# RMS norm with ReLU: two pairs of transfers merged, one wait split, and eight rows scaled on ScalarE in place of VectorE

## The chip, the cores and the metric

One core of a Trainium2 chip. The metric is the time of one execution in microseconds (us). A "faster" or "slower" needs 2%, here 3.2 us.

## The reference

```python
batch, seq, dim = 16, 1024, 512
def reference(x, gamma, eps):            # x: normal random, fp32; gamma: ones; eps: 1e-5
    rms = np.sqrt(np.mean(x ** 2, axis=-1, keepdims=True) + eps)
    return np.maximum(x / rms * gamma, 0).astype(np.float32)
```

16,384 rows of 512 numbers are read and written once: 33.55 MB in, 33.55 MB out.

## The kernel before

Each of the 128 partitions owns 128 rows. They are handled as 8 chunks of K = 16 rows (4.2 MB each over all partitions), or 16 groups of G = 8. On-chip memory has room for 6 chunks, so chunks 6 and 7 reuse the room of 0 and 1 after those are stored. SyncE issues all transfers of x and of the output in a fixed order, which is the plan of the kernel:

```python
L, S = 0, 1                      # load, store: (kind, first row, rows)
order = [(L, 0, G), (L, G, G)] + [(L, i * K, K) for i in range(1, nslots)] + [
    (S, 0, K), (S, K, K), (L, room, K), (L, room + K, K),
    (S, 2 * K, 2 * K), (S, 4 * K, 2 * K), (S, room, K),
    (S, room + K, G), (S, room + K + G, G)]
blocks = [(0, K), (K, K), (2 * K, 2 * K), (4 * K, 2 * K), (room, K), (room + K, K)]
...
for m, (kind, a, r) in enumerate(order):       # SyncE
    if m < early: continue
    if kind == S:
        if order[m - 1][0] == L:
            nc.sync.wait_ge(*((tick, 6) if a == 0 else (done, 10)))
        nc.sync.wait_ge(done, (a + r) // G)    # VectorE has finished these rows
    elif a >= room:
        take(nc.sync, sems[order.index((S, a - room, r))], 16)   # the room is free
    transfer(m)
```

The wait for `(done, 10)`: the store of chunks 2 and 3, first after the last load, is held back until ten groups, that is chunks 0 to 4, are done.

ScalarE makes the squares and their sums row by row, and a square root per group. VectorE handles chunks 0 to 2 in a loop over groups, and the rest in whole chunks: one multiply by 1/rms, one custom pass that multiplies by gamma and clips at zero.

```python
with nc.scalar.Fori(0, ngroups) as gi:         # ScalarE
    ...                                        # 8 x (Square, accumulated), then Sqrt
...
for first, last in ((3, 3), (4, 5), (6, 7)):   # VectorE
    nc.vector.wait_ge(sq, per * (last + 1 - looped))
    whole(nc.vector.reciprocal, out=rstd[:, first * K:(last + 1) * K],
          in_=rms[:, first * K:(last + 1) * K])
    nc.vector.wait_ge(sv, steps)
    for i in range(first, last + 1):
        blk = here(i * K, K)
        whole(nc.vector.tensor_tensor, out=blk, in0=blk,
              in1=rstd[:, i * K:(i + 1) * K, None].to_broadcast([P, K, d]), op=ALU.mult)
        nc.vector.wait_ge(sv, steps)
        r = G if i == nchunks - 1 else K
        for a in range(i * K, (i + 1) * K, r):
            blk = here(a, r)
            nc.vector._custom_dve(dve_ops.TENSOR_MUL_SAT, out=blk, in0=blk,
                in1=gamma_sb[:, None, :].to_broadcast([P, r, d]),
                s0=float("inf"), s1=0.0).then_inc(done, r // G)
```

## Time and profile before

| | before |
|---|---|
| time, median of the first 3 runs | 159.94 us (159.9 to 160.0) |
| span in the profile | 158.6 us |
| busy: VectorE / ScalarE / DMA queue | 85% / 54% / 98.6% |
| bytes moved | 67.1 MB, 423 GB/s over the span |
| VectorE ends / last packet ends | 151.2 / 158.1 us |

How to read the lines of the profile: DVE is VectorE, ACT is ScalarE, SPq is SyncE's queue of transfers. A row of digits cuts the span into 40 slices; 9 is a busy share of 90% or more. The line with "issue" in it is the chain: the work that ended last, followed back from wait to wait, in shares of the span. A window line gives the stretch and its length, then the busy us and number of instructions of VectorE, ScalarE and GpSimd, the granted clock, the DMA engines' share and the GB/s.

The "GB/s" and "DMA" columns of a window count a packet where it starts, so with packets of 1 to 2.4 us a window of 1 us may read 0 and the next 2.4; longer windows are safe. The costliest groups of instructions, with line, engine, operation, operands, shapes and count, then busy us and mean ns of one:

```profile
L131 ACT ACTIVATE junk<-slots 128x512 f32 x128 | 74.4, 581 | 21.7 <-POOLq L118 17.2 <-issue 4.5
L168 DVE TENSOR_TENSOR slots<-slots,rstd 128x8192 f32<-128x8192 f32 x5 | 43.4, 8689 | 0.1
L185 DVE CUSTOM_DVE_ANT_1 slots<-slots,gamma_sb 128x8192 f32<-128x8192 f32 x4 | 34.8, 8692 | 0.5
L185 DVE CUSTOM_DVE_ANT_1 slots<-slots,gamma_sb 128x4096 f32<-128x4096 f32 x2 | 8.8, 4423 | 0.0
```

A chunk costs VectorE two passes of 8.69 us, 17.4 us, and ScalarE 11.6 us. VectorE is the slower of the two, and this is what the change works on. One wait of VectorE is in VectorE's timeline (start, length, and in brackets the idle time before and what ended it):

```profile
71.03 8.69 DVE L185 CUSTOM_DVE_ANT_1 slots<-slots,gamma_sb 128x8192 f32<-128x8192 f32 x1
80.61 0.35 DVE L168 RECIPROCAL rstd<-rms 128x32 f32<-128x32 f32 x1 [0.89 <-ACT rms L136]
81.00 8.69 DVE L168 TENSOR_TENSOR slots<-slots,rstd 128x8192 f32<-128x8192 f32 x1
```

Chunk 4 waits here for chunk 5's statistics, since one reciprocal serves both.

### The profile page before, as it was taken

How to read it: one execution, taken by the hardware profiler on the slowest of the kernel's cores; microseconds unless marked ns; L12 is line 12 of the kernel's file. 1: busy time of each engine (PE TensorE's matmuls, PEld its weight loads, DVE VectorE, ACT ScalarE, POOL GpSimd, SP SyncE). 2: the span in 40 equal slices, each digit the busy share in tenths (PEclk: the TensorE clock that was granted, in tenths of full speed). 3: DMA queues.
4: the chain of work that ended last, by engine and by line, in shares of the span. 5: the costliest groups of instructions: out<-in, count | busy, mean ns of one | idle time of the engine just before them, and what ended most of it. 6: DMA issues, size and time to landing. Idle time of an engine off the chain costs nothing.

```text
span 158.6 us, 770 instructions
## 1 busy us (share of the span) xinstructions
DVE 135.2 (85%) x76; ACT 86.3 (54%) x273; POOL 0.8 (0%) x6
## 2 busy tenths in 40 slices
DVE  0014999999999999999979999999999999999910
ACT  0388929889889989988920098898600000000000
POOL 1000000000000000000000000000000000000000
DMA  6999999999999999999999999997969969999997
GB/s 190 411 450 422 512 397 397 463 463 397 405 504 413 397 413 504 405 397 463 463 397 397 446 479 397 529 463 331 529 298 496 529 264 529 397 397 397 455 405 331
DMA packets 2312, 67.12 MB, mean 423 GB/s; under 512 B 260, under 2 KB 260, under 8 KB 264
## 3 DMA queue, kind: packets, MB, share of 16 engines
q1 hardware_dynamic: 2304, 67.11, 98.6%
q10 hardware_dynamic: 8, 0.01, 0.0%
HBM read 33.56 MB, written 33.55 MB: 423 GB/s over the span
## 4 chain that ended last, share of the span: by engine, by line
DVE 44%; ACT 27%; issue 6%; ACTq 4%; DVEq 0%; POOLq 0%
ACT junk L131 26%; DVE slots L185 22%; DVE slots L168 22%; ACTq L131 3%; ACTq L126 1%; DVE rstd L168 0%; ACT rms L136 0%; ACTq L136 0%; ACTq L139 0%; DVEq L181 0%; POOLq L118 0%
## 5 line engine op out<-in xcount | busy, mean ns | idle before, releaser
L131 ACT ACTIVATE junk<-slots 128x512 f32 x128 | 74.4, 581 | 21.7 <-POOLq L118 17.2
L185 DVE CUSTOM_DVE_ANT_1 slots<-slots,gamma_sb 128x8192 f32<-128x8192 f32 (+1 forms) x6 | 43.5, 7269 | 0.6
L168 DVE TENSOR_TENSOR slots<-slots,rstd 128x8192 f32<-128x8192 f32 x5 | 43.4, 8689 | 0.1
L154 DVE SCALAR_TENSOR_TENSOR slots<-slots,rstd,gamma_sb 128x512 f32 x48 | 32.3, 747 | 0.9 <-DVE rstd L149 0.9
L131 ACT ACTIVATION_READ_ACCUMULATOR junk<-slots x128 | 23.9, 187 | 0.0
L161 DVE TENSOR_SCALAR slots<-slots x6 | 13.8, 2294 | 0.2
L142 DVE LOAD_MASK_SELECT gamma_sb<-gseed x1 | 0.0, 14 | 8.2 <-DMA gseed<-in_gamma_dram 8.2
L136 ACT ACTIVATE rms<-ss,eps_sb x16 | 4.8, 301 | 1.8
L149 DVE RECIPROCAL rstd<-rms x6 | 1.2, 196 | 5.1 <-ACT rms L136 5.1
L124 ACT ACT_TABLE_LOAD x1 | 1.3, 1283 | 4.0 <-issue 4.0
L168 DVE RECIPROCAL rstd<-rms 128x32 f32<-128x32 f32 (+1 forms) x3 | 0.9, 315 | 0.9 <-ACT rms L136 0.9
L142 DVE STREAM_SHUFFLE gamma_sb<-gseed 128x512 f32<-128x512 f32 x1 | 0.7, 721 | 0.0
L113 POOL MEMSET gseed<- 128x512 f32 x1 | 0.5, 524 | 1.9 <-POOLq L98 1.9
L214 POOL MEMSET const-uint8-127<- 128x1 uint8 x1 | 0.1, 102 | 0.0
L214 POOL MEMSET const-bfloat16-1.0<- 128x1 bf16 x1 | 0.1, 101 | 0.0
L214 POOL MEMSET const-float32-0.0<- 128x1 f32 x1 | 0.1, 98 | 0.2 <-issue 0.2
L114 POOL MEMSET eps_sb<- 128x1 f32 x1 | 0.1, 99 | 0.0
L214 POOL MEMSET const-float32-1.0<- 128x1 f32 x1 | 0.1, 98 | 0.0
## 6 DMA issues: line engine op xcount, KB each, us to landing
slots<-in_x_dram SPq DMA_DIRECT2D x7, 4096.0 KB, 29.6
out_dram<-slots SPq DMA_DIRECT2D x3, 4096.0 KB, 15.0
slots<-in_x_dram SPq DMA_DIRECT2D x2, 2048.0 KB, 9.5
out_dram<-slots SPq DMA_DIRECT2D x2, 2048.0 KB, 7.1
out_dram<-slots SPq DMA_DIRECT2D x2, 22.2
gseed<-in_gamma_dram ACTq DMA_DIRECT2D x1, 8.0 KB
```

The costliest lines, as they stand in the source:

```text
L113: nc.gpsimd.memset(gseed, 0.0).then_inc(sem_z, 1)
L124: nc.scalar.preload_act_table(ACTF.Sqrt)
L126: with nc.scalar.Fori(0, ngroups) as gi:
L131: a = nc.scalar.activation(out=junk[:, j, :], in_=slots[:, bass.ds(base + j * d, d)], func=ACTF.Square, accum_out=ss[:, bass.ds(col + j, 1)])
L136: nc.scalar.activation(out=rms[:, bass.ds(col, G)], in_=ss[:, bass.ds(col, G)], func=ACTF.Sqrt, bias=eps_sb, scale=inv_d).then_inc(sq, 1)
L142: nc.vector.stream_shuffle(gamma_sb, gseed, [0] * 32)
L149: nc.vector.reciprocal(out=rstd[:, bass.ds(col, G)], in_=rms[:, bass.ds(col, G)]).then_inc(sv, 1)
L154: r = nc.vector.scalar_tensor_tensor(out=row, in0=row, scalar=rstd[:, bass.ds(col + j, 1)], in1=gamma_sb, op0=ALU.mult, op1=ALU.mult)
L161: nc.vector.tensor_scalar_max(out=blk, in0=blk, scalar1=0.0).then_inc(done, 1)
L168: emit(**kw).then_inc(sv, 1)
L185: nc.vector._custom_dve(dve_ops.TENSOR_MUL_SAT, out=blk, in0=blk, in1=gamma_sb[:, None, :].to_broadcast([P, r, d]), s0=float("inf"), s1=0. ...
L214: nc = _bacc.Bacc("TRN2", target_bir_lowering=False, num_devices=1)
```

## The change

The intent is fewer, larger transfers and less work on VectorE at the end. Chunks 4 and 5 load together; VectorE takes each as soon as its own statistics are there; the last 16 rows leave in one store; ScalarE, idle by then, scales the last 8 rows.

```diff
-    order = [(L, 0, G), (L, G, G)] + [(L, i * K, K) for i in range(1, nslots)] + [
+    order = [(L, 0, G), (L, G, G)] + [
+        (L, K, K), (L, 2 * K, K), (L, 3 * K, K), (L, 4 * K, 2 * K),
         (S, 0, K), (S, K, K), (L, room, K), (L, room + K, K),
-        (S, 2 * K, 2 * K), (S, 4 * K, 2 * K), (S, room, K),
-        (S, room + K, G), (S, room + K + G, G)]
+        (S, 2 * K, 2 * K), (S, 4 * K, 2 * K), (S, room, K), (S, room + K, K)]
 ...
-    for first, last in ((3, 3), (4, 5), (6, 7)):
+    half = rows - G
+    for first, last in ((3, 3), (4, 4), (5, 5), (6, 7)):
 ...
+        if last == nchunks - 1:
+            nc.scalar.wait_ge(sv, steps)
+            for a in range(half, rows):
+                row = here(a, 1)
+                m = nc.scalar.activation(out=row, in_=row, func=ACTF.Identity,
+                                         scale=rstd[:, a:a + 1])
+            m.then_inc(am, 1)
         for i in range(first, last + 1):
 ...
+            r = K
+            if i == nchunks - 1:
+                r = K - G
+                nc.vector.wait_ge(am, 1)
             (multiply of r rows in place of K; one custom pass of K rows in place of two of G)
```

More of the change, by code (lines that the diff above doesn't have):

```diff
@@ L71 @@
     sv = nc.alloc_semaphore("sv")
+    am = nc.alloc_semaphore("am")
     def here(a, r):
@@ L175 @@
         nc.vector.wait_ge(sv, steps)
+        if last == nchunks - 1:
[5 more added lines that the diff above has]
+            m.then_inc(am, 1)
         for i in range(first, last + 1):
             blk = here(i * K, K)
-            whole(nc.vector.tensor_tensor, out=blk, in0=blk,
-                  in1=rstd[:, i * K:(i + 1) * K, None].to_broadcast([P, K, d]),
+            r = K
+            if i == nchunks - 1:
+                r = K - G
+                nc.vector.wait_ge(am, 1)
+            whole(nc.vector.tensor_tensor, out=blk[:, :r, :], in0=blk[:, :r, :],
+                  in1=rstd[:, i * K:i * K + r, None].to_broadcast([P, r, d]),
                   op=ALU.mult)
             nc.vector.wait_ge(sv, steps)
-            r = G if i == nchunks - 1 else K
-            for a in range(i * K, (i + 1) * K, r):
-                blk = here(a, r)
-                nc.vector._custom_dve(
-                    dve_ops.TENSOR_MUL_SAT, out=blk, in0=blk,
-                    in1=gamma_sb[:, None, :].to_broadcast([P, r, d]),
-                    s0=float("inf"), s1=0.0).then_inc(done, r // G)
+            nc.vector._custom_dve(
+                dve_ops.TENSOR_MUL_SAT, out=blk, in0=blk,
+                in1=gamma_sb[:, None, :].to_broadcast([P, K, d]),
+                s0=float("inf"), s1=0.0).then_inc(done, per)
     take(nc.sync, done, ngroups)
@@ L193 @@
     take(nc.sync, sv, steps)
+    take(nc.sync, am, 1)
     take(nc.sync, sem_g, 16)
```

## The prediction

> **What bounds the kernel now.** I read the page's slices first, since they show which unit is never idle, then the DMA queue, and the chain last.
>
> ```profile
> DVE 135.2 (85%) x76; ACT 86.3 (54%) x273; POOL 0.8 (0%) x6
> DVE  0014999999999999999979999999999999999910
> DMA  6999999999999999999999999997969969999997
> q1 hardware_dynamic: 2304, 67.11, 98.6%
> DVE 44%; ACT 27%; issue 6%; ACTq 4%; DVEq 0%; POOLq 0%
> ```
>
> VectorE is busy 85% and the chain that ended last names it with 44% and ScalarE with 27%, so one could take VectorE for the bound. But its slices start in the third of forty and end two slices before the DMA's, while the one DMA queue in use fills 98.6% of the time of all 16 engines. The 7s and 6s in the DMA row are an artefact: a packet is booked where it starts. The window view over longer stretches (the column before the last is the DMA share, the last GB/s) shows no hole:
>
> ```profile
> 12.00:60.00 48.00, 44.86 (x60) 41.17 (x133) 0.00 (x0) 1.00 1.01 437
> 60.00:99.00 39.00, 37.77 (x8) 26.55 (x86) 0.00 (x0) 1.00 1.00 430
> 99.00:138.00 39.00, 38.71 (x6) 13.72 (x45) 0.00 (x0) 1.00 0.99 430
> 138.00:148.00 10.00, 9.96 (x3) 0.00 (x0) 0.00 (x0) 1.00 0.99 426
> 148.00:158.00 10.00, 3.15 (x1) 0.00 (x0) 0.00 (x0) 1.00 0.97 413
> ```
>
> From 12 to 148 us the share is 0.99 to 1.01 at 426 to 437 GB/s. Following the packets one by one, I find 16 always in flight from about 2.2 us until the last ends at 158.1 us, and no engine idle for more than 0.18 us between two of them. So the bound is the byte count, 67.1 MB, and the chain is misleading here: it starts from the last instruction that waited, but that wait ends with a store that stood in line behind other stores.
>
> How much room is there at the end? The timeline of the last 26 us:
>
> ```profile
> 125.06 8.69 DVE L185 CUSTOM_DVE_ANT_1 slots<-slots,gamma_sb 128x8192 f32<-128x8192 f32 x1
> 133.67 8.68 DVE L168 TENSOR_TENSOR slots<-slots,rstd 128x8192 f32<-128x8192 f32 x1
> 133.78 17.73 SPq L83 DMA_DIRECT2D out_dram<-slots  x3
> 142.38 8.76 DVE L185 CUSTOM_DVE_ANT_1 slots<-slots,gamma_sb 128x4096 f32<-128x4096 f32 x2
> ```
>
> The three stores there are issued at 133.78, 146.84 and 151.17 us, each as VectorE finishes. The trace has the store of chunk 6 landing on its 16 engines at 148.3 to 148.8 us, so the first half store has stood in line for 1.4 us when the engines reach it; it lands at 153.2 to 153.7, so the second half store has stood for 2.0 us.
>
> **What the Trainium skill says.** "DMA: Bandwidth & Descriptors", section "Where 436 GB/s comes from", gives 16 ports x 32 bytes x 850 MHz = 435.2 GB/s as the ceiling. The trace agrees: packets of 65,536 bytes take 2.418 us, that is 16 x 65,536 / 2.418 us = 433.6 GB/s. The same page, section "Anatomy of one DMA", calls the semaphore write's bubble tiny; the trace has 256 such records of 7 to 9 ns. "ScalarE: Activation LUTs", section "Table sets: the hidden batching unit", has identity in every set, so the new scaling should need no second table load; the trace of before has one load, 1.28 us, for Square and Sqrt together, and can't show Identity. "SBUF — State Buffer", section "SBUF: two separate sides", says that ScalarE has its own port and that DMA and engines don't contend. The trace agrees: VectorE's 128x8192 multiply took 8.69 us at 62.2 us beside ScalarE and 8.69 us at 81.0 us beside none.
>
> **The change, part by part.**
>
> *Packets.* In the trace, medians by packet size are 0.611 us for 16,384 bytes, 1.213 for 32,768 and 2.418 for 65,536. Doubling saves 2 x 0.611 - 1.213 = 0.009 us, and 2 x 1.213 - 2.418 = 0.008 us: about 9 ns of fixed cost a packet. Each engine carries 8 of a transfer's 128 partition rows.
> - Chunks 4 and 5 in one load: 16 packets of 1.213 become 8 of 2.418 per engine, 19.408 - 19.344 = 0.06 us less.
> - The last 16 rows in one store: 16 of 0.611 become 8 of 1.213, 9.776 - 9.704 = 0.07 us less.
> - Two transfers fewer, so two semaphore writes of 9 ns fewer per engine: 0.02 us.
> All of it lies on the path, as the engines never rest: 0.15 us off.
>
> *The merged load.* Chunk 4's rows now land with chunk 5's, at 61.4 instead of 51.8 us. ScalarE began chunk 4 only at 57.8 us, being behind, so it loses about 4 us: 61.4 + 0.4 (landing to first square, as at 22.6 to 23.0) = 61.8. It then ends group 9 near 73.2 and group 11 near 84.5 us (5.79 us a group). VectorE is on chunk 3 until 79.7, so group 9 is in time. The change also splits VectorE's wait: chunk 4 waits for group 9 only, which removes the wait for group 11 (0.89 us in the trace before the reciprocal at 80.61). One reciprocal more costs some 0.2 us. Chunk 5 starts at 97.6, long after 84.5. ScalarE idles from 80.6 to 91.0 us today, waiting for chunk 6's landing, so the 4 us end in that hole: group 12 starts at 91.0 as before.
>
> *The tail on VectorE.* It multiplies 8 rows instead of 16 in chunk 7. Half of the 8192-wide multiply costs about what the custom pass on 4096 does, 4.42 us, so 8.69 - 4.42 = 4.27 us are saved; one custom pass of 8.69 instead of two of 4.42 saves 0.15. With 0.9 gained and 0.3 lost above, VectorE should end at 151.2 - 5.0 = 146.2 us.
>
> *ScalarE's new part.* Eight instructions on 128x512. The squares take 0.58 us each, so 8 x 0.6 = 5 us, from 115.4 (the reciprocal of chunks 6 and 7) to about 120.5. VectorE needs them at 132.9. Hidden.
>
> *The sum.* None of the compute gain reaches the end, unless a store is late. Stores of chunks 2 and 3, issued at 98.5 before, come at 97.5, while the engines finish chunk 7's load at 99.6 to 100.3. Chunks 4 and 5: 115.2 against a line that lasts to 119.3. Chunk 6: 133.0 against 138.6. The last store: 146.2 against 148.1. Issue to first packet needs about 1.0 us (0.73 to 1.74 at the start, 98.54 to 99.60 later, without a hole). The smallest spare is then 1.9 us, against 1.4 before. So 159.94 - 0.15 = 159.79 us.
>
> **The rivals.**
>
> *The saved VectorE time shows: about 155 us (5 us less).* For it speak the chain, with VectorE at 44%, and its unbroken work from 81 to 151 us. Against it: the DMA share of 0.97 to 1.01 in every stretch. After VectorE's end, 4.2 MB are still to go out in one store, which alone takes 9.70 us: were the line empty at 146.2, its last packet would end at 146.2 + 1.0 + 9.7 = 156.9 on the trace's clock, only 1.2 us before the 158.1 of today; with the line lasting to 148.1 it is 157.9.
>
> *The single last store is late: 161 us or more.* The last store can't start before all 16 rows are done. Without the ScalarE help VectorE would end at 146.2 + 4.3 = 150.5 us, and with the 1 us of issue the store would start 3.4 us after the line has run dry at 148.1. So this needs ScalarE's share to fail: if its group 15 or the reciprocal slipped, or if the Identity pass took over 17 us instead of 5. The squares' rate speaks against that.
>
> *The merged load opens a hole.* If chunk 4's results came over 2 us late, the stores of chunks 2 and 3, held back until then, would leave the DMA idle at 100 us. It would take group 9 beyond 82 us, and I have it at 73. Likewise the first store doesn't depend on chunk 4: it is issued at 58.4, 3 us before the loads end.
>
> *Larger packets are slower on loads.* 65,536-byte packets occur only in stores today. In 32,768-byte packets loads and stores cost the same, so I see no reason for it; 10% more on that load would be 1.9 us.
>
> **Range and chances.** The working gives 159.8. The runs of before spread over 0.1 us and another chip may shift both kernels by some tenths, hence 159.45 to 160.15. Over 2% is 3.2 us: faster would need a byte rate that the trace never shows, slower a hole of 3 us in the line; 1% and 2%.
>
> **What the profile of after would show.** Right: a DMA share of 1 to the end, 2016 records in the queue instead of 2304 (14 transfers of 128 rows, 1792, and 14 x 16 semaphore writes, where 16 transfers gave 2048 + 256), VectorE ended near 146 us, eight ScalarE instructions of about 0.6 us by 121 us, no second table load, and the wait before chunk 4's reciprocal gone. Wrong: a DMA slice well below 9 near 61, 99 or 148 us, a load packet of 64 KB over 2.5 us, or VectorE waiting for ScalarE before the last multiply.

## The result, and the profile after

The changed kernel took 159.96 us (median of 6 runs, 159.66 to 160.18) against 159.97 us (6 runs, 159.9 to 160.29) for the kernel before. The ratio is 0.9996, with a 95% interval of 0.9983 to 1.0009: the same. Ratios are the mean time of one kernel's fast runs over that of the other's of the same rounds, so not quite the ratio of the medians.

First the page of the changed kernel, busy shares, slices, queue and chain:

```profile
DVE 130.9 (83%) x76; ACT 91.3 (58%) x281; POOL 0.8 (0%) x6
DVE  0014999999999999999999999999999999998000
DMA  6999999999999699999999999997989969999996
q1 hardware_dynamic: 2016, 67.11, 98.5%
DVE 64%; issue 9%; ACT 3%; DVEq 2%; ACTq 0%; POOLq 0%
```

VectorE's row now has three empty slices at the end instead of one, yet the span is the same 158.6 us. The 6 in the DMA row, at 51.5 to 55.5 us, comes from counting the larger packets where they start; the windows below have no hole there. The queue handles 2016 records instead of 2304, as predicted, and fills nearly the same share. The chain's shares changed wildly, from VectorE 44% and ScalarE 27% to 64% and 3%, while the time did not: two such chains are no measure of what a faster engine would bring.

The windows of the kernel after, in the same stretches as in the prediction:

```profile
12.00:60.00 48.00, 44.83 (x60) 38.97 (x126) 0.00 (x0) 1.00 1.01 437
60.00:99.00 39.00, 38.62 (x9) 28.80 (x92) 0.00 (x0) 1.00 1.00 430
99.00:138.00 39.00, 38.58 (x7) 18.71 (x53) 0.00 (x0) 1.00 0.99 430
138.00:148.00 10.00, 8.14 (x1) 0.00 (x0) 0.00 (x0) 1.00 1.05 452
148.00:158.00 10.00, 0.00 (x0) 0.00 (x0) 0.00 (x0) 1.00 0.90 387
```

Up to 138 us the rates are equal to the last digit. After that 1.05 and 0.90 average to what 0.99 and 0.97 averaged to; only the packets' starts fall differently. No stretch has a hole. The last two stretches show what was gained and where it went: VectorE worked 3.15 us after 148 us before, and none now.

VectorE's timeline from chunk 4 on, and ScalarE's new part:

```profile
79.67 0.25 DVE L169 RECIPROCAL rstd<-rms 128x16 f32<-128x16 f32 x1
79.95 8.69 DVE L169 TENSOR_TENSOR slots<-slots,rstd 128x8192 f32<-128x8192 f32 x1
...
115.47 5.01 ACT L182 ACTIVATE slots<-slots,rstd 128x512 f32<-128x512 f32 x8 [1.70 <-DVE rstd L169]
115.47 8.69 DVE L169 TENSOR_TENSOR slots<-slots,rstd 128x8192 f32<-128x8192 f32 x1
124.30 8.69 DVE L195 CUSTOM_DVE_ANT_1 slots<-slots,gamma_sb 128x8192 f32<-128x8192 f32 x1
132.91 4.42 DVE L169 TENSOR_TENSOR slots<-slots,rstd 128x4096 f32<-128x4096 f32 x1
137.45 8.69 DVE L195 CUSTOM_DVE_ANT_1 slots<-slots,gamma_sb 128x8192 f32<-128x8192 f32 x1
```

The 0.89 us of waiting at 79.7 us is gone, ScalarE's eight rows are done at 120.5 us, and VectorE never waits for them. VectorE ends at 146.15 us (before: 151.15), and the last store is issued at 146.17 us. It then stands in line until the store of chunk 6 is out, which lands at 148.2 to 148.9 us.

### The profile page after: what moved, and what is told of

Read it like the earlier page. It is cut to its first block, busy times and chain, and to the rows that moved or that the text cites. A ratio compares the mean times of both kernels' runs of the same rounds, so it can differ in the third digit from the quotient of the medians.

```text
span 158.6 us, 775 instructions
## 1 busy us (share of the span) xinstructions
DVE 130.9 (83%) x76; ACT 91.3 (58%) x281; POOL 0.8 (0%) x6
## 3 DMA queue, kind: packets, MB, share of 16 engines
q1 hardware_dynamic: 2016, 67.11, 98.5%
## 4 chain that ended last, share of the span: by engine, by line
DVE 64%; issue 9%; ACT 3%; DVEq 2%; ACTq 0%; POOLq 0%
DVE slots L195 27%; DVE slots L169 25%; DVE slots L155 11%; ACT junk L132 3%; DVEq L155 1%; DVE rstd L169 1%; DVE rstd L150 1%; ACTq L132 0%; DVEq L145 0%; ACT rms L137 0%; DVEq L150 0%; DVE slots L162 0%; DVEq L194 0%; DVEq L164 0%; ACTq L137 0%
## 5 line engine op out<-in xcount | busy, mean ns | idle before, releaser
L195 DVE CUSTOM_DVE_ANT_1 slots<-slots,gamma_sb 128x8192 f32<-128x8192 f32 x5 | 43.5, 8692 | 0.7
L169 DVE TENSOR_TENSOR slots<-slots,rstd 128x8192 f32<-128x8192 f32 (+1 forms) x5 | 39.2, 7837 | 0.1
L182 ACT ACTIVATE slots<-slots,rstd 128x512 f32<-128x512 f32 x8 | 5.0, 709 | 1.7 <-DVE rstd L169 1.7
L169 DVE RECIPROCAL rstd<-rms 128x16 f32<-128x16 f32 (+1 forms) x4 | 1.1, 270 | 0.0
```

Of the source, the lines that this page charges most:

```text
L169: emit(**kw).then_inc(sv, 1)
L182: m = nc.scalar.activation(out=row, in_=row, func=ACTF.Identity, scale=rstd[:, a:a + 1])
```

## The experiments

Two theories were put against each other. The **line theory** is the prediction's: the 16 DMA engines always have a transfer waiting, so VectorE's 5 us are spare, and a change shows only if it makes a store late. The **cancelling theory**: VectorE's chain does set the end, and the change is level only because the merged transfers cost what ScalarE's help brings. The page's chain and VectorE's 85% speak for it.

The custom VectorE pass could not be used in the experiments. All of them have this stand-in, which gives the same result as long as gamma is not negative (here it is 1):

```diff
-    nc.vector._custom_dve(dve_ops.TENSOR_MUL_SAT, out=blk, in0=blk,
-        in1=gamma_sb[...], s0=float("inf"), s1=0.0)
+    nc.vector.scalar_tensor_tensor(out=blk, in0=blk, scalar=0.0,
+        in1=gamma_sb[...], op0=ALU.max, op1=ALU.mult)
```

### The stand-in: both kernels with it

> The kernel before with the custom VectorE pass replaced by a scalar_tensor_tensor (max with 0, times gamma; the same result as gamma is all ones), because the custom form can't be run again here. Control for all later runs. Both theories: the replacement also reads two operands, so about 8.7 us per 128x8192 as the custom pass, and the time stays within 0.3 us of 159.95.

> The changed kernel with the same replacement. Both theories: within 0.3 us of the control, as the changed kernel was of the kernel before; VectorE ends near 146.2 us. If it differs from the control by more, the replacement is no fair stand-in.

The control (the kernel before with the stand-in) took 160.14 us, ratio 0.9995 (0.9978 to 1.0011) to the kernel before; the changed kernel with it 160.06 us, ratio 0.9988 (0.9971 to 1.0005). The stand-in passes took 8692 ns on 128x8192, as the custom ones did. VectorE ended at 151.15 and 146.04 us. The stand-in is fair.

### ScalarE's help alone

```diff
   (in words:)
+  ScalarE scales the last 8 rows, VectorE multiplies 8 rows of chunk 7 in place of 16 (as in the change)
   (separate loads of chunks 4 and 5, joint wait, two half stores: as before)
```

> The control plus ScalarE's scaling of the last 8 rows alone: load of chunks 4 and 5, their joint wait and the two half stores stay. VectorE ends some 4.3 us earlier, at about 146.9 us. Line theory (the DMA engines always have a store waiting, so VectorE's time is spare): 159.9, no change within 0.3 us. Cancelling theory (VectorE sets the end, and the changed kernel is only level because the merged transfers cost what the help gains): about 155.6.

160.32 us, ratio 1.0000 (0.9983 to 1.0017). VectorE ended at 146.81 us, 4.3 us earlier, and the time did not move; 155.6 is refuted. The windows of this run:

```profile
99.00:138.00 39.00, 38.76 (x6) 19.19 (x55) 0.00 (x0) 1.00 0.99 431
138.00:148.00 10.00, 8.78 (x3) 0.00 (x0) 0.00 (x0) 1.00 0.98 424
148.00:158.00 10.00, 0.00 (x0) 0.00 (x0) 0.00 (x0) 1.00 0.97 413
```

VectorE is idle in the last 10 us where it worked 3.15 us before, and the engines still moved 413 GB/s, as before.

### VectorE's work cut further

```diff
+            if i in (4, 5, 6):
+                r = 1          # multiply 1 row only: wrong on purpose
```

> The changed kernel with the multiplies of chunks 4, 5 and 6 cut to 1 row each (wrong result on purpose, all transfers as they were). Three multiplies fall from 8.69 to 0.69 us; VectorE should end near 137 instead of 146.2 us (it then has to wait for the last group of squares at 114 us). Line theory: 159.9, no change within 0.3 us. Cancelling theory: about 9 us less, 151.

160.38 us, ratio 1.0005 (0.9985 to 1.0024). (The comparison of results let it pass: with normal random rows 1/rms is near 1, I take it. It is not a correct kernel.) The page and the windows:

```profile
DVE 107.0 (67%) x76; ACT 91.3 (57%) x281; POOL 0.8 (0%) x6
...
99.00:138.00 39.00, 22.91 (x6) 18.80 (x53) 0.00 (x0) 1.00 1.00 431
```

24 us of VectorE work were gone, VectorE ended at 136.9 us, 9.1 us before the changed kernel's with the stand-in, and the engines moved the same 431 GB/s. The cancelling theory falls. VectorE is busy 85% and does not set the end.

### The single last store without ScalarE's help

```diff
-        (S, room + K, G), (S, room + K + G, G)]
+        (S, room + K, K)]
 ...
-            r = G if i == nchunks - 1 else K
+            r = K
```

> The control with the last 16 rows in one store (and one last VectorE pass in place of two), without ScalarE's help. The store is issued when VectorE ends, at about 151.0 us. Line theory: the stores before it are through at 148.1, issue to first packet takes 1.05 us, so the engines rest for 151.0 + 1.05 - 148.1 = 3.9 us and the time is about 163.8. If a store's size alone mattered: 159.8.

163.61 us, ratio 1.0221 (1.0204 to 1.0238): slower. The windows around the last store:

```profile
146.00:148.00 2.00, 2.00 (x1) 0.00 (x0) 0.00 (x0) 1.00 0.65 279
148.00:150.00 2.00, 2.00 (x1) 0.00 (x0) 0.00 (x0) 1.00 0.00 0
150.00:152.00 2.00, 1.13 (x1) 0.00 (x0) 0.00 (x0) 1.00 0.15 66
152.00:154.00 2.00, 0.00 (x0) 0.00 (x0) 0.00 (x0) 1.00 1.08 459
```

Here the hole is plain to see: nothing starts from 148 to 150 us, next to nothing until 152. Packet by packet the engines rested 3.93 us on average, against 3.9 expected: chunk 6's packets ended at 148.11 us on average, the store was issued at 151.16, its first packets started at 151.99 to 152.14.

### The merged load, with the joint wait and with separate waits

```diff
   merge_only and merge_split:
-    ... [(L, i * K, K) for i in range(1, nslots)] ...
+    ... (L, K, K), (L, 2 * K, K), (L, 3 * K, K), (L, 4 * K, 2 * K), ...
   merge_split only:
-    for first, last in ((3, 3), (4, 5), (6, 7)):
+    for first, last in ((3, 3), (4, 4), (5, 5), (6, 7)):
```

> The control with chunks 4 and 5 loaded in one transfer, VectorE's joint wait for both chunks kept. Line theory: ScalarE ends the squares of chunk 5 near 84.5 us instead of 80.6, VectorE waits for them from 79.7, so the store of chunks 2 and 3 is issued near 102.4 instead of 98.5 us, the loads before it are through at about 99.9, and the engines rest for some 3.5 us: 163.4. If the merged load were harmless by itself: 159.9.

> The control with the merged load and VectorE waiting for chunk 4 and for chunk 5 separately. Line theory: chunk 4's squares are done near 73.2 us, before VectorE is free at 79.7; no hole; 159.9 within 0.3 us. If the merged load itself, not the joint wait, made the hole of the run with the merged load alone: 163.4.

The merged load alone: 163.62 us, ratio 1.0226 (1.0209 to 1.0243), slower. With separate waits: 160.14 us, ratio 1.0009 (0.9992 to 1.0026), the same. First VectorE's timeline in the run with the joint wait, then its windows:

```profile
71.08 8.69 DVE L186 SCALAR_TENSOR_TENSOR slots<-slots,gamma_sb 128x8192 f32<-128x8192 f32 x1
84.70 0.35 DVE L169 RECIPROCAL rstd<-rms 128x32 f32<-128x32 f32 x1 [4.93 <-ACT rms L137]
```

```profile
98.00:100.00 2.00, 2.00 (x1) 2.00 (x7) 0.00 (x0) 1.00 0.61 262
100.00:102.00 2.00, 2.00 (x1) 2.00 (x7) 0.00 (x0) 1.00 0.00 0
102.00:104.00 2.00, 2.00 (x2) 1.52 (x6) 0.00 (x0) 1.00 1.23 524
```

The wait before chunk 4's reciprocal grew from 0.89 to 4.93 us, the store of chunks 2 and 3, which waits for chunk 4, was issued at 102.61 instead of 98.5 us, and the engines rested 3.75 us around 101 us. That wait shows at 84.7 us, the hole 16 us later, and neither near the load that caused them. With separate waits chunk 4 needs only its own statistics, and there is no hole.

So the change is two pairs. Each merged transfer, alone, costs 2.2%; each has a partner (the split wait, ScalarE's help) that makes room for it. The second pair was run only as part of the whole change.

### How much is spare before the last store

```diff
+            if i == nchunks - 1:       # repeat the pass over 4 rows (or 1); the result stays
+                again = here(i * K, 4)
+                whole(nc.vector.scalar_tensor_tensor, out=again, in0=again, scalar=0.0,
+                      in1=gamma_sb[...], op0=ALU.max, op1=ALU.mult)
+                nc.vector.wait_ge(sv, steps)
```

> The changed kernel (with the replaced pass) with a pass over 4 rows of chunk 7 done a second time just ahead of the last one (no change of the result, 2.3 us plus 0.1 of VectorE). The last store is issued near 148.6 instead of 146.2 us. Line theory: of the 2.4 us, about 0.9 is spare (146.2 + 1.05 against 148.1), so the time rises by about 1.5 us to 161.4. Cancelling theory: by 2.4, to 162.3. If more is spare than I read: less than 0.5.

> As the run with a second pass over 4 rows, but over 1 row: 0.8 us more of VectorE, the last store issued near 146.9. That lies within the 0.9 us that I read as spare, so line theory: no change within 0.2 us against the changed kernel. If there were no spare: 0.8 more, 160.9.

One row: 160.15 us, ratio 0.9996 (0.9981 to 1.0012): no change, though the store was issued 0.8 us later than in the first run of the changed kernel with the stand-in (146.87 against 146.07). Four rows: 160.94 us, ratio 1.0055 (1.0039 to 1.0072): the same by the 2% rule, but clear of the noise, 0.9 us more and not the 1.5 I expected. The windows of the run with four rows:

```profile
146.00:148.00 2.00, 2.00 (x1) 0.00 (x0) 0.00 (x0) 1.00 0.68 295
148.00:150.00 2.00, 0.51 (x1) 0.00 (x0) 0.00 (x0) 1.00 0.61 262
150.00:152.00 2.00, 0.00 (x0) 0.00 (x0) 0.00 (x0) 1.00 1.23 524
```

The hole was there: packet by packet the engines rested 1.34 us on average. Why the time grew by less comes next.

### The 0.15 us, and the engine that ends last

> The changed kernel with the replaced pass once more, five rounds, for the 0.15 us that the first runs could not resolve. Line theory with equal engines: 0.15 us below the control of the same call. Line theory with drifting engines (in the runs so far the first engine's end moved by about 0.15 us, but the last engine came 0.5 to 1.4 us after it, differently in each run, and the last one sets the time): the mean may come out lower by 0.15, but the spread of some 0.2 us between runs may still hide it.

> The control once more, on the same chip, five rounds: 160.1 within 0.2 us. Its profile should show the first engine's last landing near 158.05 us, against about 157.9 in the changed kernel.

Changed kernel 160.25 us (ratio to before 1.0000, 0.9987 to 1.0014), control 160.15 us (1.0001, 0.9988 to 1.0015). Over both calls, 9 runs each, the means are 160.15 and 160.16 us with a scatter of 0.16 us from run to run. A gain of 0.15 us is neither shown nor quite excluded.

The trace records when each of the 16 engines reports its part of a store as landed. For the last store in each profiled run:

| run | first engine | last engine | apart | time of that run |
|---|---|---|---|---|
| before | 158.02 | 158.56 | 0.54 | 159.92 |
| control, two runs | 158.10, 158.11 | 158.87, 158.54 | 0.76, 0.43 | 160.23, 159.91 |
| help alone | 158.07 | 159.14 | 1.06 | 160.49 |
| after | 157.85 | 158.56 | 0.71 | 159.92 |
| changed with stand-in, two runs | 157.91, 157.89 | 158.97, 158.80 | 1.06, 0.91 | 160.33, 160.16 |
| one row repeated | 157.88 | 158.81 | 0.93 | 160.17 |
| merged load, separate waits | 157.91 | 158.64 | 0.73 | 160.00 |
| VectorE cut | 158.13 | 159.56 | 1.43 | 160.92 |
| four rows repeated (hole) | 159.46 | 159.66 | 0.20 | 161.02 |
| single store alone (hole) | 162.09 | 162.26 | 0.18 | 163.62 |
| merged load alone (hole) | 162.10 | 162.28 | 0.18 | 163.64 |

Three readings. The time is the last engine's landing plus 1.35 to 1.37 us in each run. Without the merged load the first engine ends at 158.02 to 158.11 us, with it at 157.85 to 157.91; the run with VectorE cut, at 158.13, is an exception. But the last engine comes 0.4 to 1.4 us later, differently each time, and it alone counts: from the first four runs of the table to the next four (the changed kernel and one row repeated), the mean landing moved from 158.08 to 157.88 us for the first engine, from 158.25 to 158.12 for the average of the 16, and from 158.78 to 158.78 for the last. "DMA: Bandwidth & Descriptors", section "Why a DMA increments its semaphore by 16 and not by 1", says of a DMA that it runs on up to 16 engines "that finish independently"; the table shows by how much.

The three runs with a hole have the engines only 0.2 us apart. In the run with four rows repeated they were 0.92 us apart when chunk 6's store landed and 0.20 after the hole: the late engine spent the hole catching up. This is where the missing 0.6 us are: against the changed kernel the first engine moved by 159.46 - 157.91 = 1.55 us, just what I expected, and the last by 159.66 - 158.97 = 0.69 (by 0.86 against the second profiled run of the changed kernel, whose last engine was at 158.80).

Where the engines drift apart can be read, though not why. In the trace of before, the packets that took over 0.04 us more than the median of their size lie at the start (20 of 40) and from 78 to 81 us (13), where the line changes from stores to the load of chunk 6; few are elsewhere. In the run with VectorE cut 15 more lie from 96 to 99 us, where one store (issued at 89.49) already waited behind the last load, and the engines went from 0.48 to 1.41 us apart there. No run varied this by itself, so the cause stays open.

### The cost of a packet

```diff
+    piece = 4     # rows; each transfer is issued in pieces, waits count 16 * r // piece
 ...
+        for o in range(a, a + r, piece):
+            there = (out2 if kind == S else x2)[...][:, o - first:o - first + piece, :]
+            made.append(nc.sync.dma_start(...).then_inc(sems[m], 16))
```

> The changed kernel (with the replaced pass) with each transfer cut into pieces of 4 rows, issued one after the other with the same waits: packets of 8192 bytes instead of 16 to 64 KB. It measures the one term of the sum that should have shown, a fixed 9 ns a packet. A packet of 8192 bytes should take (0.611 + 0.009) / 2 = 0.310 us; 512 of them per engine are 158.7 us against 155.1 now, and 50 more semaphore writes of 9 ns add 0.45: 4.0 us more, 163.9. If packets had no fixed cost: 160.0 to 160.4. If the gain of larger packets is real but below the spread of the runs, this shows it enlarged.

163.28 us, ratio 1.0190 (1.0173 to 1.0207): clear of the noise, but the interval has the 2% line inside it, so by the rule unclear. It is some 3.0 us more than the kernel before, where I expected about 4 more than the changed one. The queue of this run:

```profile
q1 hardware_dynamic: 9216, 67.11, 98.9%
```

9216 records are 8192 packets and 1024 semaphore writes. The fixed cost is real, but smaller than I took it. A packet of 8192 bytes took 0.309 us in its record, as worked out; but the records of one engine overlap a little (from 12 to 140 us some 16.2 were in flight on 16 engines, against 16.04 in the changed kernel with the stand-in), so the sum of the records overstates the time. By landings of the first engine, a load of 4.2 MB took 24.95 to 34.88 = 9.93 us in small pieces against 22.32 to 32.04 = 9.72 in the changed kernel with the stand-in; less 3 semaphore writes of 9 ns that is (0.21 - 0.03) / 24 = 7.6 ns for each packet more. The store of chunks 4 and 5 took 123.53 to 143.14 = 19.61 us (up to the first piece of the next store) against 119.30 to 138.59 = 19.29; less 7 writes, (0.32 - 0.06) / 56 = 4.6 ns. Part of the 3.0 us is drift: the first engine ended at 160.32 us, 2.4 later than in that run of the changed kernel, and the last at 161.98, 3.0 later.

## Why the prediction was right, point by point

- **The bound.** Right, and shown, not only argued: 4.3 us less of VectorE (help alone) and 24 us less (VectorE cut) moved the time by nothing that the runs resolve, and each hole made in the line came out as time, less what the late engines caught up: holes of 3.93, 3.75 and 1.34 us made the runs 3.6, 3.6 and 0.9 us longer than the kernel before. The 435.2 GB/s that the prediction cites from "DMA: Bandwidth & Descriptors", section "Where 436 GB/s comes from", is the figure for the ports; for transfers between HBM and SBUF the same section says that the memory side, about 358 GB/s for a core, binds, which the prediction left out, and the 423 GB/s of this one core lie above it.
- **VectorE ends near 146.2 us; ScalarE's part is hidden.** Measured 146.15; eight rows in 5.01 us, done at 120.5 (each took 0.71 us in its record, not 0.6, but they overlap). There is one table load in the trace, so Identity needed no other.
- **The merged load.** Landed at 61.0 to 61.5 us (predicted 61.4), first square at 61.83 (61.8), reciprocal of chunk 4 at 79.67 (79.7), store of chunks 2 and 3 at 97.50 (97.5). The joint wait run confirmed the reverse: had the change not split the wait, it would have cost 2.2%. The prediction worked out the split's gain of 0.9 us but did not say that the split is what makes the merged load harmless. One of its signs of being wrong appeared without harm: 3 of the 128 load packets of 64 KB took over 2.5 us (up to 2.64), at 58.2 us; in other runs with the merged load it was none to seven.
- **Spare before the last store.** Predicted 1.9 us between issue and turn, of which about 1.0 is needed until the first packet. The "1.4 before" beside it is a misreading: the smallest spare of the kernel before was at the store of chunks 2 and 3, issued at 98.54 us with the first packet at 99.60. That is 1.06, about what an issue needs, so next to nothing was left there, and the joint wait of the merged load showed at once. Measured: 0.8 us later cost nothing, 2.4 us later opened a hole of 1.34. Issue to first packet was 0.83 to 0.98 us in the three runs with a hole.
- **The 0.15 us.** This step fell short, though inside the range. The saving itself is there. By the mean landing of the 16 engines, chunks 4 and 5 took 19.42 to 19.44 us to load in the four profiled runs of the kernel before, the control and help alone, and 19.35 to 19.37 in the runs with the merged load: 0.07 less, as predicted. The last 16 rows took 9.69 to 9.74 us in two stores (the same four runs and the merged load with separate waits) and 9.65 to 9.67 in one store without a hole: some 0.05 less, of 0.08 predicted. What failed is "All of it lies on the path, as the engines never rest: 0.15 us off": the sum was made for an average engine, which did land 0.12 us earlier, and the time is set by the slowest of 16, which drifts by more than that from run to run. The range, 0.7 us wide, would have held without this term, so the hit says nothing for it.
- **Nine nanoseconds a packet.** Mis-sized when carried to many packets: 7.6 ns on loads, 4.6 ns on stores by landings.

- **Slips that change nothing.** VectorE's row ends one slice before the DMA's, not two; the reciprocal is said to cost 0.2 us and then counted as 0.3; 148.1 + 9.7 is 157.8, not 157.9. The two multiplies compared under "SBUF" speak for ScalarE only, as transfers ran beside both; for the transfers, the last VectorE pass of the run with the single store alone took 8.69 us too, though the engines rested during its last 3 us.

None of the experiments points to a version that beats both kernels. The packets of the changed kernel need 155.14 us an engine by their medians, the first starts at 1.74 us and the last ends at 158.09.

## What to carry to other kernels

Look at the queue of transfers before the busiest engine: when 16 engines are always served from a line that is never empty, a compute saving is spare time, and only a transfer that is issued too late is felt (here stores; a late load was not tried). Spare time can still be spent: here it pays for a merged transfer that would otherwise cost 2.2%, so judge the parts of a change alone as well as together. And a gain worked out for the average of 16 engines can be seen in the time only if it is larger than the drift between them.

## What the Trainium skill lacked or had wrong

- "DMA: Bandwidth & Descriptors": it says that the 16 engines finish independently, but not how far apart they drift under a full line: 0.43 to 1.43 us at the end of these kernels (1.66 with small packets), 0.18 to 0.20 us after a hole in the line. Which engine is late these traces do not tell.
- "DMA: Bandwidth & Descriptors", section "Latency and other measured facts", gives about 600 ns to the first byte for a transfer issued from SyncE or ScalarE. It does not say from which moment. From the start of the issue to the first packet these runs show 0.83 to 0.98 us with idle engines, and from the end of the issuing instruction, 0.33 to 0.34 us later, 0.50 to 0.65: no contradiction, but 600 ns from the start would be too little.
- "DMA: Bandwidth & Descriptors" has a fixed cost of a packet for small transfers, but no page gives it apart for loads and stores: with packets of 8 KB, 7.6 ns for loads and 4.6 ns for stores by landings, while the packets' own records would suggest 9.
